# Layer 0 of a four-layer trunk: all 2048 features of the gate product accumulate K chunk by K chunk in eight banks, with shift and scale mostly from VectorE

## The chip, the cores and the metric

The kernel runs on one core of one Trainium2 chip. The metric is the device time of one execution in microseconds (us), taken from outside the profile. Three runs of the kernel before the change took 1386.49, 1388.17 and 1388.37 us; the median is 1388.17.

A core has engines that run their own instruction streams in order and wait for one another by semaphores. In the profile PE is TensorE (matmuls; PEld is its loading of the stationary operand), DVE is VectorE, ACT is ScalarE, POOL is GpSimd, and SP is SyncE, which here only issues DMAs. ACT issues a few DMAs too.

## The reference

The reference is a trunk of four layers on 256 tokens of width 1024. Each layer is a token mixer and a gated FFN with a short convolution. Ahead of each of them stands an RMS norm whose result is scaled and shifted by numbers that a vector c gives through a matrix (`ada_w`). Layer 0 and layer 3 use the gMLP mixer. What matters here is the beginning of layer 0:

```
def rmsnorm(x, g):
    y = xf * lax.rsqrt(jnp.mean(xf * xf, axis=-1, keepdims=True) + EPS)
    return (y * g)
def modulate(h, shift, scale):
    return h * (1.0 + scale[:, None, :]) + shift[:, None, :]

c_act = jax.nn.silu(c)
mod = c_act @ ada_w[i] + ada_b[i]
sh1, sc1, g1, sh2, sc2, g2 = jnp.split(mod, 6, axis=-1)
h = modulate(rmsnorm(x, mix_norm_g[i]), sh1, sc1)

def gmlp_mixer(h, w_in, ln_g, ln_b, w_s, b_s, w_out):
    z = jax.nn.gelu(h @ w_in)
    u, v = jnp.split(z, 2, axis=-1)
    v = layernorm(v, ln_g, ln_b)
    v = v.reshape(B, n, GM_CHUNK, GM_GROUPS, GM_GROUP_DIM)
    ws = jnp.where(mask[None], w_s, jnp.zeros_like(w_s))
    sv = jnp.einsum('gts,bnsgd->bntgd', ws, v) + b_s.T[None, None, :, :, None]
    y = u * sv.reshape(B, S, GM_INNER)
    return y @ w_out
```

`w_in` is 1024 x 4096: u and v have 2048 features each. Shift and scale of the first norm, `sh1` and `sc1`, are 2048 numbers, dot products of c_act with 2048 columns of `ada_w`.

## The kernel before

Activations lie with features on the 128 partitions: x is 8 chunks of 128 features by 256 tokens. Weights stream in units of 1 MB, 128 x 2048, called `raw`. Each half of a unit is split into a rounded part `wh` (a CAST on ACT, L207) and the remainder `wl` (a subtraction on DVE, L208). Each activation is likewise split into `hh` (ACT, L444) and `hlo` (DVE, L445). A product is then three matmuls: hh with wh, hh with wl, hlo with wh (`mm3`, L237).

*The start.* x comes in two halves by SP's queue; cin (c with features on partitions), a piece of the parameters prm, and sel come by ACT's queue. PE runs twelve warmup matmuls. The squares of x are taken by DVE and, for chunks 3 and 7, by ACT (`SQACT`); PE sums them (st), ACT takes the root (sdn, which needs a table load, triggered ahead by a dummy called warm), DVE the reciprocal (rsn), and PE spreads it over all partitions (bcn). For each chunk c of layer 0, `ada_first` (L326) brings 1 MB of `ada_w` and multiplies it on PE with c_act: 32 small matmuls named adaf, 64 in the trace. `first_store` transposes their result on DVE and adds the bias; `mod_post` makes amul = (1 + scale) * g from it. `modulate_chunk` (L438 to L445) then computes nt = x * amul * bcn on DVE, hh on ACT and hlo on DVE. The order of all this in layer 0 is written out by hand in `FIRST` (L39): a is an ada chunk, v a K chunk of the gate product, d a load, p a group of small loads, among them the 512 KB of cbc (c in every partition, with its Silu).

*The gate product.* v has tokens on partitions: 2 halves of 128 tokens by 4 blocks of 512 features, so eight results of 128 x 512, each one bank of PSUM. There are four banks named acc, three named misc and one for ada. `proj_tok_first` (L522) accumulates the first 1024 features K chunk by K chunk in the four acc banks, as the chunks of hh come up. The other two blocks follow with `proj_tok` when all of hh is there. Each result goes through gelu on ACT into v0 or v1, with the sum over features beside it.

*The layer norm of v.* From the sums of three blocks a shift nsh is made; the squares of v (named jk, L575) go through ACT. Gb, ws and bs (layer norm gain, the spatial weights and their bias) are loaded by ACT's queue; POOL spreads the single rows of Gb and bs over the partitions and masks ws (affine select). DVE computes variance, root and reciprocal (vrs), scales ws with it (wsp), and multiplies v with Gb (L623). rsum on PE is a row sum of ws.

*u and go.* Eight units of u follow on PE. To each belongs sv, eight small matmuls of wsp with v (L638), and on DVE gt, u and yl, with `gr`; `go` is the product with w_out, each unit of which adds to x (`residual`) and goes into the sums of squares for the FFN's norm.

*What sets the order.* The program is written engine by engine in one sequence, and a scheduler then fixes each engine's order; `issue_after` holds it at places. The rest of the ada tensors (parts 2 to 5 of layer 0, and all of the other layers) are spread over the program: those in `ADA_P` are adaps matmuls on PE, which also serve as fillers where PE would wait for a norm; those in `ADA_D` are two products per MB on DVE (L315, one custom instruction each, listed as CUSTOM_DVE_ANT_0 in the trace and as ISA in the order). `pace` and `RATE` (L50) say how many of either are loaded per weight unit in each stage. `modulated` (L449) is the norm ahead of all later blocks.

Of the kernel before, what the change touches and what calls it, by code (L numbers as in the profile page):

```python
# [8 lines left out]
F32 = mybir.dt.float32  # L9
# [8 lines left out]
D = 1024  # L18
# [20 lines left out]
FIRST = "a0 d v0 a1 a2 d v1 a3 v2 a4 d v3 a5 v4 a6 d v5 a7 v6 p v7"  # L39
# [10 lines left out]
RATE = {("mix", 0): (0.05, 0.4), ("u", 0): (0.1, 0.9), ("go", 0): (0.35, 0.7), ("up", 0): (0.05, 0.05),  # L50
# [41 lines left out]
def build(ctx, tc, A, out, stages=None):  # L92
# [65 lines left out]

    def late_c():
        with tc.issue_after(state["lastdma"]):  # L160
            nc.sync.dma_start(cbc[:], A["cb"])
        act.activation(cbc[:], cbc[:], AF.Silu)
# [107 lines left out]
    adaps = pp.tile([P, 2, 256], F32, tag="ada", name="adaps", bufs=1)  # L270
# [6 lines left out]
    def ada_tensor(l, u):  # L277


        def load(i):  # L280
# [3 lines left out]
            def run():  # L284
                h = ADA_P.index((l, u)) % 2
                ps = adaps[:, h, :]
# [39 lines left out]
    def ada_first(l, c):  # L326

        raw = wp.tile([P, KC, 4, 64], F32, tag="raw", name=f"adaf{c}", bufs=NRAW)
        nc.sync.dma_start(raw[:].rearrange("p a b c -> p (a b c)"), A["ada0"][l, c])
        ps = misc(f"adaf{c}", (P, 64))  # L330
        with contextlib.ExitStack() as es:
            if "pe" in firsts:
                es.enter_context(tc.issue_after(firsts["pe"]))
            for kc in range(KC):
                for j in range(4):
                    i = pe.matmul(ps[32 * j : 32 * j + 32, :], crep(kc), raw[:, kc, j, :], start=kc == 0, stop=kc == KC - 1,
                                  tile_position=(0, 32 * j))
            firsts["pe"] = getattr(i, "ins", i)
        firsts[c] = ps

    def first_store(l, c):
        tr = t1(f"adaft{c}", 64)
        dve.transpose(tr[:], firsts[c][:])
        for e in range(2):
            b = 8 * e + c
            dve.tensor_tensor(mod[:, l, b : b + 1], tr[:, 32 * e : 32 * e + 1], prm[:, col("ada_b", l * 48 + b) : col("ada_b", l * 48 + b) + 1],
                              op=ALU.add)
        mod_post(l, 8 + c, 1)
# [158 lines left out]
    def proj_tok(blocks, name, sink, b0=0):  # L507

        for b in range(b0, blocks):
# [10 lines left out]
            for t in range(2):  # L520
                sink(b, t, ps[t])

    def proj_tok_first(name, sink, start=None):

        ps = [acc(f"{name}{i}") for i in range(4)]

        def chunk(kc):
            if kc % 2 == 0:
                firsts["w"] = unit(1, 0) if start else unit(2)
# [780 lines left out]
```

## Time and profile before

| | before |
|---|---|
| runs (us) | 1386.49, 1388.17, 1388.37 |
| profiled execution, its own time (us) | 1391.3 |
| its span in the profile (us) | 1389.6 |
| mean granted clock of TensorE | 0.995 |
| first v matmul (us from the span's start) | 11.81 |
| first matmul of u0, end of the v product (us) | 71.29 |
| last go matmul of layer 0 starts (us) | 172.34 |
| first matmul of the FFN's up product in layer 0 (us) | 177.74 |

The profiled execution is a run of its own; its span is the time between the first and the last thing recorded in it. In the rows that follow, a group's row has the line and engine, the operation, out<-in with shapes, the count, then busy us and mean ns, and behind the second bar the idle time of the engine just before these instructions with what ended it. A timeline row has the start, the duration, the engine (ACTq and SPq are the DMA queues of ACT and SP) and the line.

### The profile page before, as it was taken

How to read it: one execution, taken by the hardware profiler on the slowest of the kernel's cores; microseconds unless marked ns; L12 is line 12 of the kernel's file. 1: busy time of each engine (PE TensorE's matmuls, PEld its weight loads, DVE VectorE, ACT ScalarE, POOL GpSimd, SP SyncE). 2: the span in 40 equal slices, each digit the busy share in tenths (PEclk: the TensorE clock that was granted, in tenths of full speed). 3: DMA queues.
4: the chain of work that ended last, by engine and by line, in shares of the span. 5: the costliest groups of instructions: out<-in, count | busy, mean ns of one | idle time of the engine just before them, and what ended most of it. 6: DMA issues, size and time to landing. Idle time of an engine off the chain costs nothing.

```text
span 1389.6 us, 29284 instructions
## 1 busy us (share of the span) xinstructions
PE 1358.8 (98%) x12372; PEld 1286.1 (93%) x12372; DVE 1091.6 (79%) x1760; ACT 770.8 (55%) x1201; POOL 17.2 (1%) x17
## 2 busy tenths in 40 slices
PE   8999999999999999999989999999999999999997
PEld 6799999999987899999987889999987999999997
DVE  5699698889786698897788879889764964888853
ACT  3764366664465566654655646665456653666633
POOL 0100000000000000000010000000001000000000
PEclk9999999999999999999999999999999999999999
DMA  9869955468775276589475577558737465455531
GB/s 383 330 249 337 379 189 214 178 215 346 324 273 213 98 263 245 211 331 372 173 271 194 235 281 296 194 208 322 254 125 258 178 217 182 151 184 182 183 122 31
DMA packets 49483, 326.23 MB, mean 235 GB/s; under 512 B 5956, under 2 KB 9028, under 8 KB 11974
## 3 DMA queue, kind: packets, MB, share of 16 engines
q1 hardware_dynamic: 47568, 322.72, 61.9%
q8 instruction: 97, 1.59, 0.5%
q10 hardware_dynamic: 1784, 1.65, 0.4%
q14 instruction: 34, 0.28, 0.1%
HBM read 323.29 MB, written 1.05 MB: 233 GB/s over the span
## 4 chain that ended last, share of the span: by engine, by line
PE 92%; DVE 3%; DMA 3%; ACT 2%; issue 1%; DVEq 0%; SPq 0%; ACTq 0%
PE up L239 12%; PE up L238 12%; PE up L240 12%; PE dn L238 4%; PE dn L239 4%; PE dn L240 4%; PE go L238 2%; PE go L239 2%; PE go L240 2%; PE u L239 2%; PE u L238 2%; PE u L240 2%; PE adaps L293 2%; PE v L238 2%; PE v L239 2%; PE v L240 2%
## 5 line engine op out<-in xcount | busy, mean ns | idle before, releaser
L207 ACT CAST wh<-raw 128x1024 fp32r<-128x1024 f32 x426 | 434.9, 1031 | 395.5 <-PE up L239 171.4
L208 DVE TENSOR_TENSOR wl<-raw,wh 128x1024 fp32r<-128x1024 f32 x426 | 511.7, 1206 | 162.9 <-ACT wh L207 160.9
L238 PE MATMUL up<-hh,wh 128*128 128x256 f32 x1408 | 398.4, 284 | 2.6 <-ACT hh L444 2.5
L240 PE MATMUL up<-hh,wl 128*128 128x256 f32 x1408 | 398.3, 283 | 0.0
L239 PE MATMUL up<-hlo,wh 128*128 128x256 f32 x1408 | 398.2, 284 | 0.1
L238 PEld LDWEIGHTS up<-hh,wh 128*128 128x128 f32 x1408 | 270.5, 192 | 5.3 <-ACT hh L444 4.5
L239 PEld LDWEIGHTS up<-hlo,wh 128*128 128x128 f32 x1408 | 270.4, 192 | 0.6 <-DVE hlo L445 0.5
L240 PEld LDWEIGHTS up<-hh,wl 128*128 128x128 f32 x1408 | 270.8, 193 | 0.0
L238 PE MATMUL dn<-gh,wh 128*128 128x256 f32 x528 | 149.9, 284 | 1.5 <-ACT y L1089 1.5
L239 PE MATMUL dn<-gl,wh 128*128 128x256 f32 x528 | 149.4, 283 | 0.0
L240 PE MATMUL dn<-gh,wl 128*128 128x256 f32 x528 | 149.4, 283 | 0.0
L315 DVE CUSTOM_DVE_ANT_0 adaw<-adaw,cbc,prm 128x1024 f32<-128x1024 f32 x104 | 131.3, 1276 | 2.2 <-DMA adaw<-adad 2.2
L1089 ACT ACTIVATE y<-up,cwb 128x256 f32<-128x256 f32 x176 | 98.6, 560 | 10.1 <-DVE y L1091 9.8
L238 PEld LDWEIGHTS dn<-gh,wh 128*128 128x128 f32 x528 | 101.3, 192 | 2.0 <-ACT y L1089 1.7
L239 PEld LDWEIGHTS dn<-gl,wh 128*128 128x128 f32 x528 | 101.3, 192 | 0.0
L240 PEld LDWEIGHTS dn<-gh,wl 128*128 128x128 f32 x528 | 101.3, 192 | 0.0
L1091 DVE SCALAR_TENSOR_TENSOR y<-up,cwb,y 128x254 f32<-128x254 f32 x176 | 84.5, 480 | 4.7
L1090 DVE SCALAR_TENSOR_TENSOR y<-up,cwb,y 128x255 f32<-128x255 f32 x176 | 83.9, 477 | 0.8 <-ACT y L1089 0.8
L238 PE MATMUL u<-hh,wh 128*128 128x256 f32 x256 | 73.9, 289 | 0.0
L238 PE MATMUL go<-yh,wh 128*128 128x256 f32 x256 | 73.3, 287 | 0.0
L240 PE MATMUL u<-hh,wl 128*128 128x256 f32 x256 | 72.4, 283 | 0.0
L239 PE MATMUL u<-hlo,wh 128*128 128x256 f32 x256 | 72.4, 283 | 0.0
(337 smaller groups left out, 2478.8 us busy)
## 6 DMA issues: line engine op xcount, KB each, us to landing
raw<-up SPq DMA_DIRECT2D x88, 1024.0 KB, 4.8
adaw<-adad SPq DMA_DIRECT2D x52, 1024.0 KB, 8.1
adaw<-adap SPq DMA_DIRECT2D x36, 1024.0 KB, 7.5
raw<-dn SPq DMA_DIRECT2D x32, 1024.0 KB, 4.8
raw<-gmu SPq DMA_DIRECT2D x16, 1024.0 KB, 4.8
raw<-gmo SPq DMA_DIRECT2D x16, 1024.0 KB, 4.8
raw<-gmv SPq DMA_DIRECT2D x15, 1024.0 KB, 6.3
raw<-dn SPq DMA_DIRECT2D x16, 768.0 KB, 5.5
```

What stands on the lines that cost most here:

```text
L207: act.copy(wh[:, :w], raw[:, o : o + w])
L208: i = dve.tensor_tensor(wl[:, :w], raw[:, o : o + w], wh[:, :w].bitcast(F32), op=ALU.subtract)
L238: pe.matmul(ps, lh, rh, start=start, stop=False)
L239: pe.matmul(ps, lh, rl, start=False, stop=False)
L240: i = pe.matmul(ps, ll, rh, start=False, stop=stop)
L293: pe.matmul(ps[32 * j : 32 * j + 32, :], crep(kc), raw[:, k, j, :], start=kc == 0, stop=kc == KC - 1, tile_position=(0, 32 * j))
L315: dve.tensor_tensor_reduce(raw[:, e, :], raw[:, e, :], cbc[:], 1.0, prm[:, c0 : c0 + 1], ALU.mult, ALU.add, mod[:, l, b : b + 1])
L1089: act.activation(y[:], ps[:, e, :], AF.Identity, bias=b, scale=w[2])
L1090: dve.scalar_tensor_tensor(y[:, 1:], ps[:, e, : S - 1], w[1], y[:, 1:], op0=ALU.mult, op1=ALU.add)
L1091: dve.scalar_tensor_tensor(y[:, 2:], ps[:, e, : S - 2], w[0], y[:, 2:], op0=ALU.mult, op1=ALU.add)
```

## The change

Layer 0's gate product runs in one pass. All four blocks of 512 features accumulate K chunk by K chunk, in eight banks: four acc, three misc, and the bank that the ada matmuls use. So one unit of weights is now one K chunk (all 2048 columns), and gelus, squares and layer norm come when the last chunk is done (`proj_tok_all`).

Shift and scale of layer 0: chunks 0 and 1 stay on PE (`FIRSTPE = 2`). For chunks 2 to 7 the columns lie in the layout of the DVE products, and DVE takes two products of 128 x 1024 per chunk. These need c in every partition at once: one row of c (crow, 1 x 1024) is loaded by ACT's queue, goes through Silu, and POOL spreads it. The 512 KB load of cb and its Silu go. bcn is copied to SBUF (bcs), so that its bank comes free; chunks from 1 on use the copy.

In layer 0 the gating of a unit of u now runs one unit late (`lag = 1`), `pace` for u is given a count, and the rates of u and go are changed.

```diff
-FIRST = "a0 d v0 a1 a2 d v1 a3 v2 a4 d v3 a5 v4 a6 d v5 a7 v6 p v7"
+FIRSTPE = 2
-RATE = {("mix", 0): (0.05, 0.4), ("u", 0): (0.1, 0.9), ("go", 0): (0.35, 0.7), ("up", 0): (0.05, 0.05),
+RATE = {("mix", 0): (0.05, 0.4), ("u", 0): (0.1, 0.75), ("go", 0): (0.35, 0.9), ("up", 0): (0.05, 0.05),
...
     cbc = one.tile([P, D], F32, name="cbc")
-
-    def late_c():
-        with tc.issue_after(state["lastdma"]):
-            nc.sync.dma_start(cbc[:], A["cb"])
-        act.activation(cbc[:], cbc[:], AF.Silu)
+    nc.scalar.dma_start(cbc[0:1, :], A["crow"])
+    act.activation(cbc[0:1, :], cbc[0:1, :], AF.Silu)
+    pool.partition_broadcast(cbc[:], cbc[0:1, :])
...
+    def first_load(l, c):
+
+        raw = wp.tile([P, 2048], F32, tag="raw", name=f"adaf{c}", bufs=NRAW)
+        nc.sync.dma_start(raw[:], A["ada0"][l, c])
+        firsts[c] = raw
+
+    def first_run(l, c):
+        raw = firsts.pop(c)
+        if c >= FIRSTPE:
+
+            v = raw[:].rearrange("p (e k) -> p e k", e=2)
+            for e in range(2):
+                b = 8 * e + c
+                c0 = col("ada_b", l * 48 + b)
+                dve.tensor_tensor_reduce(v[:, e], v[:, e], cbc[:], 1.0, prm[:, c0 : c0 + 1], ALU.mult, ALU.add, mod[:, l, b : b + 1])
+        else:
+            v = raw[:].rearrange("p (k j f) -> p k j f", k=KC, j=4)
+            ps = ada(f"adaf{c}", (P, 64))
+            with contextlib.ExitStack() as es:
+                if "pe" in firsts:
+                    es.enter_context(tc.issue_after(firsts["pe"]))
+                for kc in range(KC):
+                    for j in range(4):
+                        i = pe.matmul(ps[32 * j : 32 * j + 32, :], crep(kc), v[:, kc, j, :], start=kc == 0, stop=kc == KC - 1,
+                                      tile_position=(0, 32 * j))
+                firsts["pe"] = getattr(i, "ins", i)
+            tr = t1(f"adaft{c}", 64)
+            dve.transpose(tr[:], ps[:])
+            for e in range(2):
+                b = 8 * e + c
+                c0 = col("ada_b", l * 48 + b)
+                dve.tensor_tensor(mod[:, l, b : b + 1], tr[:, 32 * e : 32 * e + 1], prm[:, c0 : c0 + 1], op=ALU.add)
         mod_post(l, 8 + c, 1)
 
...
+    def proj_tok_all(l, name, bc0, bc):
+
+        make = [acc] * 4 + [misc] * 3 + [ada]
+        ps = {}
+
+        def products(kc, w, blocks):
             with contextlib.ExitStack() as es:
-                if start and kc < KC - 1:
+                if "pe" in firsts:
                     es.enter_context(tc.issue_after(firsts["pe"]))
-                for b in range(2):
-                    a, bl = hl(firsts["w"], (kc % 2) * 1024 + b * 512, 512)
+                for b in blocks:
+                    a, bl = hl(w, b * 512, 512)
                     for t in range(2):
-                        mm3(ps[2 * b + t][:], hh[:, kc, t * P : t * P + P], hlo[:, kc, t * P : t * P + P], a, bl, kc == 0, kc == KC - 1)
+                        if kc == 0:
+                            ps[b, t] = make[2 * b + t](f"{name}{b}{t}", (P, 512))
+                        mm3(ps[b, t][:], hh[:, kc, t * P : t * P + P], hlo[:, kc, t * P : t * P + P], a, bl, kc == 0, kc == KC - 1)
             firsts["pe"] = state["mm"]
 
-        if start:
-            start(chunk)
-        else:
-            for kc in range(KC):
-                chunk(kc)
-        for i in range(4):
-            sink(i // 2, i % 2, ps[i])
+        modulate_chunk(l, 0, 0, bc0)
+        dma_next()
+        first_load(l, 1)
+        dma_next()
+        first_load(l, 2)
+        for kc in range(KC):
+            w = unit(2) if kc == KC - 1 else unit(1, 0)
+            if kc + 1 < FIRSTPE:
+
+                products(kc, w, (0, 1))
+                first_run(l, kc + 1)
+                products(kc, w, (2,))
+                modulate_chunk(l, 0, kc + 1, bc)
+                products(kc, w, (3,))
+            else:
+                products(kc, w, range(4))
+                if kc < KC - 1:
+                    first_run(l, kc + 1)
+                    modulate_chunk(l, 0, kc + 1, bc)
+            if kc + 2 < KC:
+                dma_next()
+            if kc + 3 < KC:
+                first_load(l, kc + 3)
+            if kc == KC - 3:
+                with tc.issue_after(state["lastdma"]):
+                    nc.sync.dma_start(prm[:, n0:n1], A["prm"][:, n0:n1])
+                conv_load(l)
+        return ps
...
+        nsh = sm("nsh", 2)
+
+        def shift():
+
+            dve.tensor_reduce(nsh[:], sums[:].rearrange("p (t q) -> p t q", t=2)[:, :, 0:3], axis=AX.X, op=ALU.add)
+            dve.tensor_scalar_mul(nsh[:], nsh[:], -4.0 / (3 * GI))
 
...
-        proj_tok_first("v", sink, start)
         if start:
-            pace("mix", l, 20)
-        proj_tok(3, "v", sink, 2)
-
-        nsh = sm("nsh", 2)
+            ps = proj_tok_all(l, "v", *start)
+            for b in range(4):
+                if b == 3:
+                    shift()
+                for t in range(2):
+                    sink(b, t, ps[b, t][:])
+
+            conv_half()
+            conv_half()
+        else:
+            proj_tok_first("v", sink)
+            proj_tok(3, "v", sink, 2)
...
         pool.partition_broadcast(bsf, bsf[0:1, :])
-        proj_tok(4, "v", sink, 3)
...
             dve.tensor_tensor(gt[:], sv[:], r[:].unsqueeze(2).broadcast_to([P, 2, 2, P]), op=ALU.add)
             dve.tensor_tensor(u[:], u[:], gt[:].rearrange("p e t s -> p e (t s)"), op=ALU.mult)
             split(yh(2 * i, 2), yl(2 * i, 2), u[:])
+
+        pace("u", l, *((16,) if start else ()))
+        us = []
+        lag = 1 if start else 0
+        for i in range(8):
+            ps = proj_pair(hk, lk, KC, f"u{i}")
+            if i == 0:
+                state["chain"] = tuple(getattr(s, "ins", s) for j, s in enumerate((warm, rec, root)) if GCH >> j & 1)
+            u = t2("u", (P, 2, S))
+            with tc.issue_after(getattr(root, "ins", root)):
+                act.activation(u[:], ps[:], AF.Gelu_apprx_tanh)
+            us.append((i, u))
+            if len(us) > lag:
+                gating(*us.pop(0))
+        for u in us:
+            gating(*u)
         pace("go", l)
...
                     quick = False
-                    ada_first(l, 0)
+                    first_load(l, 0)
+                    first_run(l, 0)
                     bc0 = rms_bc(cur["st"], D, "n0")
-
...
-                    gmlp(l, l // 3, start)
+                    bcs = big("bcs", (P, S))
+                    act.copy(bcs[:], bc0[:])
+                    gmlp(l, l // 3, (bc0[:], bcs[:]))
...
+    r["crow"] = np.ascontiguousarray(f["c"].reshape(1, D))
+
+
+    a0 = np.ascontiguousarray(aw[:1, :, :2048].reshape(1, KC, P, 2, 8, 4, 32).transpose(0, 4, 2, 1, 5, 3, 6)).reshape(1, 8, P, 2048)
```

**Where instructions now stand.** Two engines at three places, as the programs list them. The first is ACT from the start of the program to the first hh, before:

```order
L152 ACTIVATE cact<-cin 128x8
L1152 ACTIVATE sq_105<-x 128x256 x2
L1155 ACT_TABLE_LOAD
L1155 ACTIVATE warm<-sq_105 128x1
L408 ACTIVATE sdn_184<-st,epsc 128x64
L207 CAST wh_0_212<-raw_209 128x1024
L444 ACTIVATE hh<-nt,mod 128x256
```

and after:

```order
L152 ACTIVATE cact<-cin 128x8
L1220 ACTIVATE sq_107<-x 128x256
L159 ACTIVATE cbc<-cbc 1x1024
L1220 ACTIVATE sq_107<-x 128x256
L1223 ACT_TABLE_LOAD
L1223 ACTIVATE warm<-sq_107 128x1
L421 ACTIVATE sdn_191<-st,epsc 128x64
L205 CAST wh_0_219<-raw_210 128x1024
L1247 COPY bcs<-bcn_195 128x256
L205 CAST wh_1024_223<-raw_210 128x1024
L457 ACTIVATE hh<-nt,mod 128x256
```

The Silu of the row cbc has moved in between the two squares; the copy bcs and a second cast stand ahead of the first hh.

The second place is ACT behind the gate product of layer 0, from the first square jk to the gelu table for u, after:

```order
L637 ACTIVATE jk_627,ss_622<-v0_202,nsh_205 128x512
L637 ACTIVATE jk_629,ss_622<-v1_203,nsh_205 128x512
L637 ACTIVATE jk_631,ss_622<-v0_202,nsh_205 128x512
L637 ACTIVATE jk_633,ss_622<-v1_203,nsh_205 128x512
L643 DMA Gb_635<-gmg 1x2048
L648 DMA ws_638<-gmws 128x1024
L651 DMA bs_640<-gmbs 1x1024
L670 ACT_TABLE_LOAD
L670 ACTIVATE warm_657<-epsc_81 128x1
L637 ACTIVATE jk_659,ss_622<-v0_202,nsh_205 128x512
L637 ACTIVATE jk_661,ss_622<-v1_203,nsh_205 128x512
L660 COPY ws_638<-rsum_644 128x512
```

Before, the three loads stood ahead of the first square, and the last of them there read so:

```order
L591 DMA bs_768<-gmbs 1x1024
L575 ACTIVATE jk_751,ss_748<-v0_193,nsh_747 128x512
L575 ACTIVATE jk_753,ss_748<-v1_194,nsh_747 128x512
L575 ACTIVATE jk_755,ss_748<-v0_193,nsh_747 128x512
L575 ACTIVATE jk_757,ss_748<-v1_194,nsh_747 128x512
```

So the loads of Gb, ws and bs have moved from ahead of the first six squares to behind them.

The third place is DVE at the norm between layer 0's mixer and its FFN, from the last square sq to the first nt, before:

```order
L425 TENSOR_TENSOR sq<-x 128x256
L410 RECIPROCAL rsn_2072<-sdn_2070 128x64
L208 TENSOR_TENSOR wl_0_2120<-raw_1986,wh_0_2119 128x1024
L443 SCALAR_TENSOR_TENSOR nt<-x,amul,bcn_2074 128x256
L143 CAST gmask<-gm_2067 128x192
```

and after:

```order
L438 TENSOR_TENSOR sq<-x 128x256
L318 ISA adaw_4_3_1891,mod<-adaw_4_3_1891,cbc,prm 128x1024
L318 ISA mod 128x1
L423 RECIPROCAL rsn_1859<-sdn_1857 128x64
L318 ISA adaw_4_3_1891,mod<-adaw_4_3_1891,cbc,prm 128x1024
L318 ISA mod 128x1
L206 TENSOR_TENSOR wl_0_1913<-raw_1771,wh_0_1912 128x1024
L143 CAST gmask<-gm_1854 128x192
L254 SCALAR_TENSOR_TENSOR amul<-mod,prm 128x8
L206 TENSOR_TENSOR wl_1024_1941<-raw_1771,wh_1024_1940 128x1024
L456 SCALAR_TENSOR_TENSOR nt<-x,amul,bcn_1861 128x256 x3
```

Two custom products, amul and a second wl have moved in ahead of nt.

More of the change, by code (lines that the diff above doesn't have):

```diff
@@ L324, in build @@
     firsts = {}
[L326 to L333, printed above, removed]
-            for kc in range(KC):
[L335 to L339, printed above, removed]
@@ L624, in gmlp, with gating @@
         yh, yl = hilo("y", 16)
-        pace("u", l)
-        for i in range(8):
-            ps = proj_pair(hk, lk, KC, f"u{i}")
-            if i == 0:
-                state["chain"] = tuple(getattr(s, "ins", s) for j, s in enumerate((warm, rec, root)) if GCH >> j & 1)
-            u = t2("u", (P, 2, S))
-            with tc.issue_after(getattr(root, "ins", root)):
-                act.activation(u[:], ps[:], AF.Gelu_apprx_tanh)
+        def gating(i, u):
             g = i
```

65 lines of the change are left out of this document (23 added, 42 removed).

## The prediction

> **What bounds the kernel now.** I read the page first: busy times, the chain that ended last, the costliest groups.
>
> ```profile
> PE 1358.8 (98%) x12372; PEld 1286.1 (93%) x12372; DVE 1091.6 (79%) x1760; ACT 770.8 (55%) x1201; POOL 17.2 (1%) x17
> PE 92%; DVE 3%; DMA 3%; ACT 2%; issue 1%; DVEq 0%; SPq 0%; ACTq 0%
> L208 DVE TENSOR_TENSOR wl<-raw,wh 128x1024 fp32r<-128x1024 f32 x426 | 511.7, 1206 | 162.9 <-ACT wh L207 160.9
> ```
>
> TensorE is idle for 1389.6 - 1358.8 = 30.8 us. So a gain must come from work taken off TensorE or from those waits, and any new wait of TensorE costs its full length. Next the groups by line of the first 90 us (of 20 to 90 us for ACT and DVE); the first row is what the change takes off TensorE, with its waits at the row's end.
>
> ```profile
> L336 PE MATMUL adaf<-adaf,cact 128*32 128x64 f32 x512 | 8.8, 220 | 3.7 <-DMA adaf<-ada 3.7
> L443 DVE SCALAR_TENSOR_TENSOR nt<-x,amul,bcn 128x256 f32<-128x256 f32 x6 | 2.9, 480 | 0.2
> L561 ACT ACTIVATE v<-v 128x512 f32<-128x512 f32 x8 | 4.7, 595 | 5.2 <-PE v L240 5.1
> L575 ACT ACTIVATE jk<-v,nsh 128x512 f32<-128x512 f32 x8 | 5.7, 714 | 1.2 <-DVE nsh L579 1.1
> L623 DVE SCALAR_TENSOR_TENSOR v<-v,nmu,Gb 128x512 f32<-128x512 f32 x8 | 5.7, 742 | 0.0
> ```
>
> Then the timeline of the start (start, duration), the DMA answer for it (last number: us from issue to landing), and a row of the windows (last two numbers: DMA share, GB/s).
>
> ```profile
> 1.73 0.45 ACTq L131 DMA_DIRECT2D sel<-sel  x1
> 6.39 1.28 ACT L1155 ACT_TABLE_LOAD   x1
> 7.79 0.30 ACT L408 ACTIVATE sdn<-st,epsc 128x64 f32<-128x64 f32 x1
> 8.12 0.55 DVE L410 RECIPROCAL rsn<-sdn 128x64 f32<-128x64 f32 x1 [1.07 <-ACT sdn L408]
> 9.59 1.10 PE L415 MATMUL bcn<-rsn,sel 128*128 128x64 f32 x8
> 11.25 0.51 ACT L444 ACTIVATE hh<-nt,mod 128x256 fp32r<-128x256 f32 x1
> 11.81 0.74 PE L238 MATMUL v<-wh,hh 128*128 128x512 f32 x2 [1.12 <-ACT hh L444]
> cin<-c ACTq DMA_DIRECT2D x1, 4.0 KB, 3.9
> sel<-sel ACTq DMA_DIRECT2D x1, 2.0 KB, 7.0
> 30.00:40.00 10.00, 8.82 (x164) 6.63 (x166) 7.33 (x17) 5.04 (x7) 0.00 (x0) 1.00 1.02 412
> ```
>
> The small loads of ScalarE's queue share the engines with megabytes from SP's queue: cin needed 3.9, and sel, issued third, landed at 1.73 + 7.0 = 8.7. Then the timeline at the end of the gate product v and at the third unit of u:
>
> ```profile
> 71.06 0.39 PE L240 MATMUL v<-wh,hlo 128*128 128x512 f32 x1
> 71.29 0.28 PE L238 MATMUL u<-hh,wh 128*128 128x256 f32 x1
> 84.69 0.36 PE L238 MATMUL u<-hh,wh 128*128 128x256 f32 x1
> ```
>
> Matmuls of v start 0.23 apart, so a K chunk of 24 is 5.5 us. From 71.29 to 84.69 TensorE runs u0, u1 and two sv without a wait, and these 13.4 us cover the layer norm of v.
>
> **The change part by part.** *Removed.* Six of the eight adaf groups leave TensorE. 512 records are 64 a group, the 8.8 us are 1.1 each, and about 1.3 with the change of shape at both ends: 7.7 us, and at most the 3.7 of their waits with it. That is the whole possible gain.
>
> *Start.* ScalarE's queue gets a fourth load, crow, and its Silu stands ahead of the second square, the square-root table and sdn. No row shows crow. Issued at 2.2, it lands at 4.0 if it takes the 1.8 of Gb (rows below), or behind sel, at 9.0. I take 9.0, since it stands behind sel in the same queue. Silu on 1024 elements is 1.06 (row below), the square 0.4, the table 1.28, warm and sdn 0.4, rsn 0.55, bcn 1.1: bcn ends at 13.85 instead of 10.69. The copy bcs is new, and nt waits for it: 0.5 by the hh row of the same shape. With nt 0.5, a cast that now stands ahead of hh, 1.0, and hh 0.5 the first v matmul is at **15.8** against 11.81. With crow at 4.0 it would be 12.6. The broadcast of cbc on POOL lies beside this: VectorE wants cbc only at 23.8.
>
> *K chunks.* Half of chunk 0 (12 x 0.23) and adaf1 end at 19.7. VectorE then does transpose, mod, amul, nt, wl, hlo and wl for chunk 1, 4.1, to 23.8. From chunk 2 on each chunk costs it two custom products (2 x 1.2 back to back, rows below), amul 0.16, nt 0.48, hlo 0.48 and two wl of 1.2, with overlaps **5.9 us**, where TensorE needs 5.5. So VectorE sets the pace: 23.8 + 5 x 5.9 = 53.3, hh of chunk 7 is ready 3.7 later, at 57.0, and v ends at **62.5**, against 71.3. Transfers are close, but don't bind: 2.1 MB a chunk at 412 GB/s is 5.1. SP's queue now waits for crow and sel in places, and these are over by 9.
>
> *After v.* All eight gelus and squares now come behind the last chunk, and ScalarE issues Gb, ws and bs behind the sixth square. What such steps took before:
>
> ```profile
> 39.85 1.06 ACT L162 ACTIVATE cbc<-cbc 128x1024 f32<-128x1024 f32 x1
> 49.41 0.49 ACTq L583 DMA_DIRECT2D Gb<-gmg  x1
> 51.20 2.92 POOL L584 PARTITION_BROADCAST Gb<-Gb  x1 [50.17 <-DMA Gb<-gmg]
> 58.36 1.09 POOL L594 TENSOR_SCALAR_AFFINE_SELECT ws<-ws 128x1024 f32<-128x1024 f32 x1 [4.24 <-DMA ws<-gmws]
> 61.13 1.90 POOL L592 PARTITION_BROADCAST bs<-bs  x1 [1.67 <-DMA bs<-gmbs]
> 48.47 7.72 DVE L208 TENSOR_TENSOR wl<-raw,wh 128x1024 fp32r<-128x1024 f32 x5 [3.44 <-ACT wh L207]
> 58.70 0.77 DVE L579 TENSOR_SCALAR nsh<-nsh 128x2 f32<-128x2 f32 x1
> 59.39 1.27 DVE L315 CUSTOM_DVE_ANT_0 adaw<-adaw,cbc,prm 128x1024 f32<-128x1024 f32 x1
> 60.59 1.27 DVE L315 CUSTOM_DVE_ANT_0 adaw<-adaw,cbc,prm 128x1024 f32<-128x1024 f32 x1
> ```
>
> ScalarE: the gelu table from 58.0, one gelu (59.9), two casts (61.9), seven gelus at 0.58 (65.9), two casts (67.8), six squares at 0.71 (72.0). Its DMA queue may run a few instructions ahead of its compute; I take 70.0 for Gb's issue, 72.0 at the latest. It lands 1.8 later, as at 49.41 to 51.20, and the broadcast ends at 74.7; affine (1.09) and the broadcast of bs (1.90) follow. Meanwhile VectorE wants one custom product and four products of v with Gb (0.66 each back to back). Do these run beside POOL? Under the Gb broadcast five wl took 7.72 instead of 5 x 1.2, and nsh, on 2 elements a row, took 0.77 under affine: VectorE mostly stood still. I take them as exclusive; between 0 and 3.0 us hang on it. Then VectorE goes on at 75.8, behind affine: 1.2 + 2.65 + 1.9 = 81.6. From there variance 0.3, vrs 0.3, gelu table 1.28, gelu, copy and a cast give wh10 at 85.7, and the scaling of ws, two products of v and gr let wl10 end at 86.9. The third u unit could start at **86.8**. In before it started at 84.69, with one sv (0.8) fewer done: comparable is 85.5. TensorE has finished u1 at 74.0 and rsum at 78, so it waits some 6 us.
>
> Such a wait has a price of its own. The longest one of this trace, in the timeline and in windows (the third number from the end is the granted clock):
>
> ```profile
> 724.08 1.94 PE L937 MATMUL psum<-hsg,ones 128*32 128x512 f32 x8 [3.52 <-DVE hsg L953]
> 728.67 0.63 PE L240 MATMUL hi<-wh,hlo 128*128 128x512 f32 x1
> 729.10 0.63 PE L238 MATMUL hi<-wh,hh 128*128 128x512 f32 x1
> 725.00:728.00 3.00, 3.00 (x13) 1.67 (x6) 3.00 (x4) 0.00 (x0) 0.00 (x0) 0.50 1.08 415
> 730.00:732.00 2.00, 2.00 (x15) 1.10 (x14) 0.52 (x1) 1.05 (x1) 0.00 (x0) 1.00 0.22 90
> ```
>
> After 3.52 us of waiting the granted clock was 0.50, with matmuls 0.43 apart instead of 0.23, until about 730, 5.9 us after work came back. So sv0 to sv2, 2.4 us from 84.0 on, would take 4.9, and u2 starts at **88.9**. Bounds: 0, and half of 5.9, 2.9; I take 2.1. The Trainium skill, page "TensorE: Matmul & The Clock Gate", Part 1, has this as a rule: an idle window of about 3.4 us halves TensorE's clock, and some 3.4 us of sustained work give it back. By the page the loss here would be 1.3 (an estimate) and the sum 0.8 lower; this trace's half clock lasted longer.
>
> *Boundary to the first FFN.* By the new rates adaw0_4_3 is loaded later. Its two custom products now stand on VectorE among the steps of the norm, and amul, which needs them, and a second wl come ahead of nt.
>
> ```profile
> 173.18 0.42 DVE L425 TENSOR_TENSOR sq<-x 128x256 f32<-128x256 f32 x1
> 174.48 0.55 DVE L410 RECIPROCAL rsn<-sdn 128x64 f32<-128x64 f32 x1 [0.88 <-ACT sdn L408]
> 175.41 1.23 DVE L208 TENSOR_TENSOR wl<-raw,wh 128x1024 fp32r<-128x1024 f32 x1 [0.38 <-ACT wh L207]
> 176.56 0.47 DVE L443 SCALAR_TENSOR_TENSOR nt<-x,amul,bcn 128x256 f32<-128x256 f32 x1
> 177.74 0.51 PE L238 MATMUL up<-hh,wh 128*128 128x256 f32 x2
> ```
>
> The first product fits into the 0.88 of idle time but for 0.4. The second (1.2), amul (0.16) and wl (1.2) push nt, and with it hh and up, **2.9** later in all. TensorE's fillers here, the adaps, are 48 matmuls before and after, and before they lasted just until up; so the 2.9 are a wait. If the products come through ahead of sq, it is 0. At the other boundaries the fillers differ by 8 adaps (0.5 us) in either direction; I take 0, give or take 0.8.
>
> **Sum.** 88.9 - 85.5 = 3.4, and 2.9: +6.3, which is 1397.6 beside the profiled execution's own 1391.3. That execution lies 3.1 above the median of the runs, 1388.17, from which I start: **1394.5**.
>
> **Rivals.** *A: crow lands early*, 3.9 after issue like cin, at 6.1. For it: it is one row of 4 KB. Against it: sel's 7.0, on the same queue. First v at 12.9 and all that follows 2.9 earlier: +3.4, 1391.6.
>
> *B, not slower: POOL's work is ready in time.* ScalarE's queue issues Gb so far ahead of the squares that POOL is done before VectorE needs Gb. Then the last square, at 75.1, decides, and variance to wl10 add 5.3: u2 at 80.4, 5.1 earlier than before, with too short a wait for the half clock. With the boundary -2.2: 1386.0. It holds if Gb is issued by 66. Against it: at 49.41 Gb went out among the casts at its own place, not far ahead.
>
> *C: A and B together*, -2.2 - 2.9 = -5.1: 1383.1.
>
> *D: half clock at two more places.* At the start TensorE is idle from 7.5 to 10.4, while st waits for the second square, and at the FFN for 2.9; the clock may fall in both. For it: half a clock for 5.9 us takes 2.9 at the FFN, and bcn at half clock 1.0 at the start. Against it: the one fall that I see took 3.5 of waiting. +10.2, 1398.4.
>
> *E: VectorE's loop is hidden.* If 5.9 a chunk is too high and TensorE's 5.5 sets the pace, v ends 2.2 earlier: +4.1, 1392.3. Against it: the sum of the rows.
>
> **How the numbers follow.** Chances: forecast 0.36, A 0.12, B 0.16, C 0.13, D 0.15, E 0.08. A measurement of this kernel can tell about 0.2%, 2.8 us, from no change: 1385.4 to 1391.0 counts as the same. Slower: forecast, D, E and half of A (0.06), 0.65. Same: the other half of A and most of B (0.13), 0.19. Faster: C and the rest of B (0.03), 0.16. The range leaves out C and the far end of D: 1385.0 to 1399.5. The forecast's own range is 1392 to 1397.
>
> **What would show it.** The Silu of crow starting near 9 and the first v matmul near 15.8; VectorE with hardly any idle time between 24 and 53; v ending near 62.5; POOL's broadcast of Gb starting past 71; TensorE idle for about 6 us ahead of sv0 and a granted clock of 0.5 behind it; at the FFN, up starting 2.9 later after the last go matmul than before. I am wrong if crow lands by 5, if Gb is broadcast before 70, if u2 starts before 84, or if up follows go as closely as before.

## The result, and the profile after

The changed kernel takes 1405.20 us (median of four runs, 1404.86 to 1405.66), the kernel before 1388.27 beside it (four runs, 1386.49 to 1389.01): a ratio of 1.0123, 95% interval 1.0110 to 1.0135. It is slower by 16.9 us, where +6.3 was forecast, and it lies above the range's end of 1399.5. The profiled execution took 1405.02, its span is 1403.3. One run of all, 3534.68 us in the experiment with 832 columns below, was disturbed and is left out.

The page of the changed kernel, busy times (and instructions) of each engine:

```profile
PE 1362.6 (97%) x11988; PEld 1288.1 (92%) x11988; DVE 1103.6 (79%) x1766; ACT 768.0 (55%) x1201; POOL 18.2 (1%) x18
```

TensorE has 384 matmul records fewer (12372 - 11988, the six adaf groups) and yet 3.8 us more busy time, and it is idle for 1403.3 - 1362.6 = 40.7 us instead of 30.8. Fewer matmuls that are busy for longer go with the lower clock: the mean granted clock is 0.987 instead of 0.995. The longest waits of TensorE in the changed kernel (engine, line, what was waited for: total, times, longest):

```profile
PE rsum L659 <- POOL ws L655: 4.3, 1, 4.3
PE up L236 <- ACT hh L457: 4.0, 2, 2.5
PE gram L998 <- issue: 4.0, 2, 2.0
PE st L413 <- ACT sq L1220: 3.0, 1, 3.0
PE up L236 <- DVE y L1161: 2.4, 6, 0.4
PE sv L692 <- DVE wsp L680: 2.4, 1, 2.4
PE dn L236 <- DVE y L1161: 2.1, 1, 2.1
```

They lie at five places: the start (st), the end of v (rsum, sv), the first feed-forward (the 2.5 of up), layer 1's feed-forward (up and dn behind y), and layer 2's mixer (gram, which waits 3.1 in the kernel before, too). The timeline of the changed kernel (start, duration) at the first three, and two hh of the K loop:

```profile
8.98 1.05 ACT L159 ACTIVATE cbc<-cbc 1x1024 f32<-1x1024 f32 x1 [3.78 <-DMA cbc<-crow]
12.70 1.97 PE L428 MATMUL bcn<-rsn,sel 128*128 128x64 f32 x8 [0.16 <-DVE rsn L423]
16.48 0.79 PE L236 MATMUL v<-wh,hh 128*128 128x512 f32 x1 [1.81 <-ACT hh L457]
...
40.81 0.51 ACT L457 ACTIVATE hh<-nt,mod 128x256 fp32r<-128x256 f32 x1 [3.47 <-DVE nt L456]
46.68 0.51 ACT L457 ACTIVATE hh<-nt,mod 128x256 fp32r<-128x256 f32 x1 [3.46 <-DVE nt L456]
...
64.59 0.28 PE L236 MATMUL u<-hh,wh 128*128 128x256 f32 x1
...
71.83 0.23 ACTq L643 DMA_DIRECT2D Gb<-gmg  x1
76.28 2.30 POOL L644 PARTITION_BROADCAST Gb<-Gb  x1 [64.86 <-DMA Gb<-gmg]
76.94 2.58 DVE L318 CUSTOM_DVE_ANT_0 adaw<-adaw,cbc,prm 128x1024 f32<-128x1024 f32 x1 [2.74 <-DMA adaw<-adad]
78.42 2.04 POOL L655 TENSOR_SCALAR_AFFINE_SELECT ws<-ws 128x1024 f32<-128x1024 f32 x1
79.45 4.45 DVE L684 SCALAR_TENSOR_TENSOR v<-v,nmu,Gb 128x512 f32<-128x512 f32 x4
80.52 3.52 PE L659 MATMUL rsum<-ws,ones 128*128 128x512 f32 x4 [4.26 <-POOL ws L655]
85.28 0.15 DVE L677 RECIPROCAL vrs<-vrs 128x2 f32<-128x2 f32 x1
86.40 3.09 PE L692 MATMUL sv<-wsp,v 128*128 128x128 f32 x18 [2.36 <-DVE wsp L680]
...
177.90 0.48 DVE L472 SCALAR_TENSOR_TENSOR x<-go,gate,x 128x256 f32<-128x256 f32 x1 [4.58 <-PE go L238]
178.76 1.28 DVE L318 CUSTOM_DVE_ANT_0 adaw<-adaw,cbc,prm 128x1024 f32<-128x1024 f32 x1
180.43 1.19 DVE L318 CUSTOM_DVE_ANT_0 adaw<-adaw,cbc,prm 128x1024 f32<-128x1024 f32 x1
185.21 0.62 PE L236 MATMUL up<-hh,wh 128*128 128x256 f32 x3 [2.48 <-ACT hh L457]
```

The reader sees every mechanism that the prediction named: the Silu of crow at 9, the hh 5.87 us apart, the late Gb, VectorE's product of adaw stretched from 1.28 to 2.58 under POOL's broadcast, TensorE waiting twice ahead of sv, and up 7.31 us behind the last x (177.90 to 185.21). In the kernel before up came 5.08 behind it:

```profile
172.66 0.48 DVE L459 SCALAR_TENSOR_TENSOR x<-go,gate,x 128x256 f32<-128x256 f32 x1 [4.58 <-PE go L240]
```

That is 177.74 - 172.66. The windows of the changed kernel behind v and at the feed-forward (third number from the end: granted clock):

```profile
80.00:82.00 2.00, 1.48 (x2) 0.64 (x3) 2.00 (x2) 0.00 (x0) 2.00 (x2) 0.71 0.00 0
82.00:84.00 2.00, 2.00 (x3) 0.34 (x1) 2.00 (x5) 0.59 (x1) 0.17 (x1) 0.50 0.00 0
88.00:90.00 2.00, 2.00 (x11) 2.00 (x11) 2.00 (x4) 2.00 (x4) 0.00 (x0) 0.50 0.00 0
188.00:190.00 2.00, 2.00 (x11) 2.00 (x11) 2.00 (x6) 0.94 (x3) 0.00 (x0) 0.50 0.65 274
```

The clock was halved behind the waits for ws (rsum), for wsp (sv) and for hh (up). In the trace it is also halved from 9.15 to 19.39, behind the wait of st, and in windows of layers 2 and 3; behind the waits for y it is not.

Then the same milestones of both traces were set side by side, the first and the last x that a product has updated in each stage. The changed kernel is behind by 5.60 us at the first go (132.89 and 138.49), 5.24 at the last go, 8.91 at the end of layer 0's feed-forward, 10.83 and 15.25 at the ends of layer 1's mixer and feed-forward, 13.1 behind layer 2's mixer, and 13.7 at the end. So 8.9 us arise in layer 0, where 6.3 were predicted, and 4.8 behind it, where nothing was predicted. (In layer 2's mixer the changed kernel gains 2.1: the wait of 3.52 that the prediction shows there, with two windows at half clock behind it, is not in its trace.) The remaining 3.2 of the 16.9 are the kernel before's own profiled execution, 3.0 slower than the median of its runs, while that of the changed kernel stands at its median.

### The profile page after: what moved, and what is told of

It reads as the page before. It is cut to its first block, busy times and chain, and to the rows that moved or that the text cites. A ratio compares the mean times of both kernels' runs of the same rounds, so it can differ in the third digit from the quotient of the medians.

```text
span 1403.3 us, 28547 instructions
## 1 busy us (share of the span) xinstructions
PE 1362.6 (97%) x11988; PEld 1288.1 (92%) x11988; DVE 1103.6 (79%) x1766; ACT 768.0 (55%) x1201; POOL 18.2 (1%) x18
## 3 DMA queue, kind: packets, MB, share of 16 engines
q8 instruction: 94, 1.54, 0.4%
## 4 chain that ended last, share of the span: by engine, by line
PE 89%; DVE 5%; ACT 2%; DMA 1%; issue 1%; ACTq 0%; DVEq 0%; SPq 0%
PE up L236 12%; PE up L237 12%; PE up L238 12%; PE dn L236 4%; PE dn L237 4%; PE dn L238 4%; PE go L236 2%; PE go L237 2%; PE go L238 2%; PE adaps L296 2%; PE u L236 2%; PE u L237 2%; PE u L238 2%; DVE wl L206 2%; PE v L236 1%
```

## The experiments

Each is timed against the kernel before, whose median was 1389.0 to 1389.3 in the three batches. The changed kernel was not timed again beside them; "less than the changed kernel" is against its 1405.20, when the kernel before took 1388.27.

**The start: crow first on ScalarE's queue.**

```
+    cbc = one.tile([P, D], F32, name="cbc")
+    nc.scalar.dma_start(cbc[0:1, :], A["crow"])
     cin = one.tile([P, 8], F32, name="cin")
...
-    cbc = one.tile([P, D], F32, name="cbc")
-    nc.scalar.dma_start(cbc[0:1, :], A["crow"])
     act.activation(cbc[0:1, :], cbc[0:1, :], AF.Silu)
```

> Only change against the changed kernel: crow is issued first on ScalarE's queue instead of fourth. Theory (the start is paid because the Silu of crow holds the second square): crow lands by about 4.5, its Silu runs from about 4.8 to 6.2, first v matmul at about 12.9 instead of 16.48, the granted clock stays full through the first 20 us, and adaf1 ends about 5 us earlier; as the K chunks go at VectorE's pace, everything behind follows: about 1400.2, 5 us less than the changed kernel's 1405.2 (3.4 to 6). Rival (the later stages are held by something with a time of its own, the transfers of the weights or of adaw0_2_1): the first v matmul moves as far, but u2 by less than 2 us, 1403 or more.

Measured: 1403.29 (1400.44 to 1405.36), ratio 1.0107 (1.0087 to 1.0127): 1.9 less than the changed kernel. Its timeline:

```profile
4.02 1.06 ACT L159 ACTIVATE cbc<-cbc 1x1024 f32<-1x1024 f32 x1
13.85 0.79 PE L236 MATMUL v<-wh,hh 128*128 128x512 f32 x1 [1.94 <-ACT hh L457]
18.70 0.63 PE L238 MATMUL v<-wh,hlo 128*128 128x512 f32 x1
19.26 1.27 PE L352 MATMUL adaf<-adaf,cact 128*32 128x64 f32 x64
```

The Silu comes 5 us earlier and the first v 2.6 earlier, but the second chunk's adaf only 1.5 earlier (19.26 instead of 20.78): all of chunk 0's products now run at half clock (each takes 0.63; in the changed kernel they take 0.39 from 19.5 on). v ends 1.3 earlier, vrs also 1.3, go's first x 1.6, but the third unit of u only 0.7 (88.48 instead of 89.14). So the theory holds for the first v alone. The full clock that it counted on did not come: this trace has half clock from 12.85 to 19.68, and again from 77.70 to 87.94. Total and third unit of u lie where the rival put them, but its reason is not borne out, since vrs moves by as much as the end of v: nothing with a time of its own held it there. The 1.9 in total are not clear of noise by themselves: the intervals of the two ratios overlap.

**After v: Gb, ws and bs issued behind the last chunk's hh.**

```
         if start:
             ps = proj_tok_all(l, "v", *start)
+            with tc.issue_after(state["hh"]):
+                Gb, wr, ws, rsum, bs = loads()
...
+            if start and i == 1:
+                rsums()
```

`loads()` holds the three DMAs and POOL's two broadcasts, `rsums()` the row sum, now behind u1; state["hh"] is the last hh.

> Against the changed kernel: Gb, ws and bs are issued right behind the last chunk's hh instead of behind the sixth square, and rsum stands behind u1 in the program. Theory (the broadcasts on GpSimd and their quarrel with VectorE hold the third unit of u): GpSimd is done with Gb by about 66 and with bs by about 72, the eight products of v with Gb take 0.66 to 0.74 each instead of 1.1, vrs comes at about 78.2 instead of 84.79, the third unit of u starts at about 82.2 instead of 89 to 91, and there is no half clock behind it: about 1397.5, 7.5 us less (6 to 9). Rival (adaw0_2_1's landing at 76.9, for which VectorE waited, or ScalarE's chain of gelus and squares, holds it): vrs comes no earlier than 82, 1402 or more.

Measured: 1397.05 (1395.84 to 1400.39), ratio 1.0072 (1.0051 to 1.0093): 8.2 less. Its timeline:

```profile
59.02 0.23 ACTq L622 DMA_DIRECT2D Gb<-gmg  x1
63.53 2.55 POOL L623 PARTITION_BROADCAST Gb<-Gb  x1 [51.98 <-DMA Gb<-gmg]
71.95 1.28 DVE L318 CUSTOM_DVE_ANT_0 adaw<-adaw,cbc,prm 128x1024 f32<-128x1024 f32 x1
74.20 3.40 DVE L698 SCALAR_TENSOR_TENSOR v<-v,nmu,Gb 128x512 f32<-128x512 f32 x5
79.23 0.16 DVE L691 RECIPROCAL vrs<-vrs 128x2 f32<-128x2 f32 x1
79.96 2.05 PE L706 MATMUL sv<-wsp,v 128*128 128x128 f32 x16 [1.45 <-DVE wsp L694]
```

Confirmed. With POOL done by 69 VectorE's product takes 1.28 again and a v product 3.40 / 5 = 0.68 instead of 4.45 / 4 = 1.11; sv starts at 79.96 instead of 86.40, and from v to the boundary (177.4) no window is at half clock. The Trainium skill, page "SBUF — State Buffer", section "Who interferes with whom", states that a VectorE instruction with two inputs in SBUF contends with a GpSimd instruction that reads SBUF, for a port pair that is locked exclusively. The two traces agree as far as the lengths go (2.58 and 1.28, 1.11 and 0.68). Gb still takes 63.53 - 59.02 = 4.5 from issue to broadcast, as in the changed kernel (76.28 - 71.83).

**The clock after v: TensorE kept busy.**

```
+            if start and i == 1:
+                keep = ada("keep", (P, P))
+                with tc.issue_after(state["mm"]):
+                    for n in range(36):
+                        pe.matmul(keep[:], onesw[:], onesw[:], start=True, stop=True)
```

> The changed kernel with 36 matmuls of the constant ones behind layer 0's u1: 27 ahead of rsum and 9 behind it, so that TensorE is busy while it waits for ws and for wsp. Theory: the half clock at 80.8 and 87.7 comes from the idle stretches of 4.3 and 2.4 us, so the granted clock stays at 1.00 from 76 to 92, sv still starts at 86.4 +- 0.5, and what follows it gains the 1.7 us that half of a 3.41 us window costs: u2's milestones and go0 1.7 earlier, 1403.5. Rival 1: the clock falls without idleness, the same windows at 0.50, 1405 to 1406. Rival 2: the clock stays up here but the window turns up later, so the total is within 0.5 of 1405.2.

Measured: 1401.70 (1400.44 to 1402.88), ratio 1.0093 (1.0080 to 1.0106): 3.5 less. Its windows and its timeline:

```profile
82.00:84.00 2.00, 2.00 (x9) 1.04 (x8) 2.00 (x5) 0.59 (x1) 0.12 (x1) 1.00 0.00 0
88.00:90.00 2.00, 2.00 (x18) 1.89 (x17) 2.00 (x3) 2.00 (x3) 0.00 (x0) 1.00 0.00 0
```

```profile
76.22 6.19 PE L717 MATMUL keep<-ones 128*128 128x128 f32 x54
82.25 1.88 PE L659 MATMUL rsum<-ws,ones 128*128 128x512 f32 x4
86.36 1.83 PE L692 MATMUL sv<-wsp,v 128*128 128x128 f32 x14 [0.22 <-DVE wsp L680]
```

TensorE does 36 matmuls (72 records) more, nothing that it waits for comes earlier (sv at 86.36 and 86.40), and the kernel is faster. The clock stayed at 1.00, rsum took 1.88 instead of 3.52, and go's first x came 1.3 earlier, where 1.7 was expected. So here idleness brings the half clock. The rest of the gain lies elsewhere: behind it each stage matches the changed kernel's to within 0.5 us (1.1 together) up to layer 2's mixer, which took 152.8 instead of 156.5; there the changed kernel's trace has two windows of 3.41 us at half clock (at 763.5 and 777.1) and this one none (1.4 of it is lost again in layer 3's feed-forward, to a second window there). The shift in time changed where such windows fall; that this is a matter of phase is argued, not shown.

**What paces the K loop.** First VectorE's products were halved.

```
-                dve.tensor_tensor_reduce(v[:, e], v[:, e], cbc[:], 1.0, ...
+                dve.tensor_tensor_reduce(v[:, e, :512], v[:, e, :512], cbc[:, :512], 1.0, ...
```

> The changed kernel with VectorE's products for chunks 2 to 7 over 512 of the 1024 columns (half of each sum is left out, the loads stay as they are). VectorE then works some 4.7 us a chunk, TensorE's 24 matmuls need 5.43. Theory, VectorE paces the K loop: v ends near 62.6 instead of 64.6 (TensorE's own floor: 16.5 + 8 x 5.43 + 1.1 for the second chunk's adaf + 1.6 at half clock), about 1403.2. Rival, the loads pace it as much (two of 1 MB per 5.9 us is 355 GB/s, the DMA share reads 0.94 to 1.02 in each 6 us window from 28 to 64): v still ends between 64.2 and 64.8 and VectorE now waits for DMA, 1405.

Measured: 1408.35 (1405.92 to 1409.97), ratio 1.0140 (1.0127 to 1.0153), v ends at 65.56: neither theory. The waits of VectorE in this kernel, from 28 to 58 us:

```profile
DVE hlo L458 <- ACT hh L457: 2.9, 5, 0.6
DVE wl L206 <- ACT wh L205: 2.3, 5, 0.5
```

VectorE waits for ScalarE, never for a DMA: with the shorter products the scheduler had put hh ahead of two casts on ScalarE, and the round trip of hh, casts, wl and nt took 5.94 a chunk. The order had changed with the size, so the run could not answer. With 832 columns the order on all engines is that of the changed kernel:

> The changed kernel with VectorE's products for chunks 2 to 7 over 832 of the 1024 columns (the rest of each sum is left out, the loads stay as they are). The instructions stand in the same order on VectorE, ScalarE and TensorE as in the changed kernel, which with 512 columns they did not. Each of the twelve products takes 0.23 us less, so VectorE's own work falls from 5.87 to 5.42 us a chunk, TensorE's 24 matmuls need 5.43. Theory, VectorE paces the K loop: the hh of chunks 3 to 7 follow each other by 5.42 to 5.5 instead of 5.87, the last hh comes some 2 us earlier (56.4 instead of 58.4), v ends 1.5 to 2 earlier, and the total lies near 1403.5. Rival, the loads pace it (two of 1 MB per 5.87 us): the spacing stays at 5.8 to 5.9 and VectorE waits for DMA or ScalarE, total 1405.

Measured: 1402.11 to 1404.53 in three runs, ratio 1.0100 (1.0075 to 1.0125). Two hh of this kernel:

```profile
45.42 0.51 ACT L457 ACTIVATE hh<-nt,mod 128x256 fp32r<-128x256 f32 x1 [3.06 <-DVE nt L456]
50.90 0.51 ACT L457 ACTIVATE hh<-nt,mod 128x256 fp32r<-128x256 f32 x1 [3.07 <-DVE nt L456]
63.07 0.28 PE L236 MATMUL u<-hh,wh 128*128 128x256 f32 x1
```

5.47 apart instead of 5.87, and v ends 1.5 earlier. In the changed kernel's own trace VectorE waits for nothing from 28 to 58 us. So VectorE sets the pace in the changed kernel; rival E, that its loop is hidden, falls. (The total, 1.0100, is not clear of the changed kernel's 1.0123; the spacing is what decides.) The loads, though busy throughout, keep up with 5.47.

**Behind layer 0: the planner's accumulators.** The planner has one accumulator for each kind of ada load ("p" for TensorE's, "d" for VectorE's). Each unit adds the stage's RATE to them, and one load goes out for each whole one reached. They carry over from stage to stage. In front of layer 0's feed-forward they stand at 0.35 and 1.0 in the kernel before, at 0.15 and 0.4 in the changed one. Three kernels: the old values put back in the changed kernel; the same and the old rate for u, which brings adaw0_4_3 back ahead of the norm; and the new values alone in the kernel before.

```
             pace("up", l, 33, "big")
+            if l == 0:
+                state["p"], state["d"] = 0.34999999999999987, 0.9999999999999998
```

> Against the changed kernel: one line sets the two accumulators that pace the loads of the ada tensors, at the beginning of layer 0's FFN, to the values that they had there in the kernel before, so that from there on nearly every ada load stands where it stood before; layer 0's mixer and its boundary stay as in the changed kernel. Theory (part of the loss is scattered over layers 1 to 3, because the ada work was shifted there by these accumulators): of the 13.7 us between the two traces 4.8 arise behind layer 0's FFN, and these go: about 1400.4 (1399.5 to 1402). Rival (that part is due to where the clock's windows fall, or is the same in any kernel that starts late): 1404 or more.

```
-RATE = {("mix", 0): (0.05, 0.4), ("u", 0): (0.1, 0.75), ...
+RATE = {("mix", 0): (0.05, 0.4), ("u", 0): (0.1, 0.9), ...
```

> As the run with the accumulators set, and besides the rate of u is 0.9 instead of 0.75, so that adaw0_4_3 is loaded and multiplied ahead of the last square of layer 0's norm. Theory (VectorE's two products, amul and wl ahead of nt make the boundary 3.7 us longer, 2.5 of waiting and the rest by half clock): the time from the last go matmul to up is the 5.1 us of before, and the total is lower by 3.7 than with the accumulators alone: about 1396.7 (1395.5 to 1398). Rival (the boundary is long for another reason, hh on ScalarE or the fillers): no more than 1 us lower than with the accumulators alone.

```
             pace("up", l, 33, "big")
+            if l == 0:
+                state["p"], state["d"] = 0.15, 0.4
```

> The kernel before with one line added: the accumulators of the planner's pace stand at 0.15 and 0.4 in front of layer 0's feed-forward, as the changed kernel leaves them there, instead of 0.35 and 1.0. Up to that line it is the kernel before, word for word; behind it its loads stand as in the changed kernel. Theory: the carried accumulators cost what the stages behind layer 0's feed-forward lost in the changed kernel: +4.8, 1393.8, with layer 1's mixer +1.9 and its feed-forward +4. Rival: the loss needs the changed kernel's late boundary as well: 1389 to 1390.

Measured: 1400.28 (1396.17 to 1400.77), ratio 1.0080 (1.0061 to 1.0099), 4.9 less than the changed kernel; with the rate 1397.01 (1393.24 to 1397.79), ratio 1.0058 (1.0039 to 1.0076), 8.2 less, with up 5.08 behind the last x as in the kernel before; and the kernel before with the line 1396.64 (1392.88 to 1398.94), ratio 1.0060 (1.0048 to 1.0072): 7.5 slower, where 4.8 was expected. The first two came as their theories had them. TensorE's waits and groups in layer 1's feed-forward, first of the kernel before (463 to 652 us):

```profile
PE up L238 <- ACT hh L444: 1.5, 1, 1.5
L293 PE MATMUL adaps<-adaw,cact 128*32 128x256 f32 x54 | 3.7, 382 | 0.0
```

then the group of the changed kernel (474 to 667 us), where all the waits behind y of its list above lie:

```profile
L296 PE MATMUL adaps<-adaw,cact 128*32 128x256 f32 x70 | 4.8, 383 | 0.6 <-DVE adat L261 0.6
```

of the changed kernel with the old values put back (474 to 661 us):

```profile
L296 PE MATMUL adaps<-adaw,cact 128*32 128x256 f32 x54 | 3.7, 382 | 0.0
```

and of the kernel before with the one line (464 to 657 us):

```profile
PE up L238 <- DVE y L1091: 2.4, 6, 0.4
PE dn L238 <- DVE y L1091: 2.1, 1, 2.1
L293 PE MATMUL adaps<-adaw,cact 128*32 128x256 f32 x70 | 4.8, 383 | 0.6 <-DVE adat L263 0.6
```

One line that touches no computation brings the changed kernel's times in layer 1 to the kernel before, and the same line with the old values takes them away again. 16 records of adaps more stand in this feed-forward, and VectorE, with the moved products of adaw on it, delivers y late to up and dn. The stage takes 191.9 us in the changed kernel and in the kernel before with the line, 187.6 in the kernel before and in the changed kernel with the old values; layer 1's mixer 90.7 against 88.8. (Both traces with 187.6 hold a window at half clock there, at 470.5 and at 481.8; the two with 191.9 hold none.) With the old values put back, the time from the end of layer 0 to the end of the program is 6.5 less than in the changed kernel's trace. The rival, that the late boundary is needed for this, falls.

What the line costs in the kernel before is less sure than that it costs. Its runs go with their clock: 1392.9 at a mean granted clock of 0.997, 1394.7 at 0.996, 1398.5 to 1398.9 at 0.993 to 0.990. At 0.997 there is one run of it, and three of the kernel before, 1387.1 to 1387.7: 5 to 6 us. Span against span the two traces differ by only 1.6, because layer 2's mixer takes 153.9 with the line and 158.7 without it, in a trace that has the wait of 3.52 and its two windows there. Where its longer runs lose their time is not shown; the one trace of it is of the shortest.

**All three repairs together.**

> The changed kernel with all three repairs at once: the c row loaded first on ScalarE's queue, Gb/ws/bs issued behind the last chunk's hh with rsum behind u1, and the accumulators and layer 0's u rate as the kernel before has them in front of the feed-forward. Theory: the four costs lie one behind the other on TensorE's path, so the gains add: 1405.2 - 1.9 - 8.2 - 8.2 = 1386.9, a little below the kernel before (1389.0); vrs near 77.2, x's first eighth behind the mixer (go0) near 130.6, up 5.1 behind the last x. Rival 1, the gains overlap (the boundary's stall and the late u2 wait for the same adaws): two thirds of the sum, 1392 to 1394. Rival 2, the K-chunk order itself costs: not below 1389.

Measured: 1385.58 (1383.88 to 1389.22, eight runs) beside 1389.10 (14 runs): ratio 0.9979 (0.9970 to 0.9989). Its timeline where v is normalised:

```profile
77.50 0.15 DVE L691 RECIPROCAL vrs<-vrs 128x2 f32<-128x2 f32 x1
78.22 2.05 PE L706 MATMUL sv<-wsp,v 128*128 128x128 f32 x16 [1.59 <-DVE wsp L694]
```

The gains add: 1386.9 was expected; vrs comes at 77.50 (77.2 expected) and sv 8.2 earlier than in the changed kernel, up comes 5.14 behind the last x, and go's first x at 130.45, 2.4 ahead of the kernel before. This version is faster than both kernels, by 3.5 us than the one before. So the K-chunk order was not what made the change slow; three things that came with it were. Both rivals fall.

## Why the prediction was wrong, point by point

The sign was right and the mechanisms of layer 0 were right; the size was 10.6 us short: 2.6 in layer 0, 4.8 behind it, and 3.2 in the starting point.

| step | predicted | measured |
|---|---|---|
| Silu of crow; first v | 9.0; 15.8 | 8.98; 16.48 |
| K loop per chunk; last hh; end of v | 5.9; 57.0; 62.5 | 5.87; 58.41; 64.59 |
| Gb issued; broadcast starts | 70.0; 71.8 | 71.83; 76.28 |
| first go against before | +3.4 | +5.6 |
| last go to the end of the first feed-forward | +2.9 | +3.7 |
| behind layer 0's feed-forward | 0 | +4.8 |
| profiled execution of before against its runs | carried over | 3.2 more |

**Start: right, mis-sized by the clock.** The order on ScalarE came as forecast, but bcn took 1.97 instead of 1.10, since the wait for st had halved the clock: the part of rival D at the start. Rivals A and C, crow early, fall with the Silu at 8.98. Chunk 0's products and adaf1 took 5.4 (16.48 to 21.88) where 3.9 were counted (15.8 to 19.7), also at half clock. The two, 0.7 and 1.5, make up v's delay of 2.1, less 0.1 that the loop won.

**K loop: right.** The pace is VectorE's, as the run with 832 columns shows.

**After v: right, mis-sized in the transfer, and near in one number by luck.** That POOL and VectorE hold each other up, with "between 0 and 3.0" hanging on it, is borne out. But the landing of Gb was taken at 1.8 us from one row, and it is 4.5 here and in the experiment: the row of before (issued at 49.41, broadcast at 51.20) was no price for it. The issue came at 71.83, near the late bound of 72.0. So the broadcast ended at 78.6 instead of 74.7. The first sv came at 86.40, where the working had 84.0. Yet u2 came at 89.14, where 88.9 was forecast: three sv at half clock, 4.9 us, were to run ahead of u2, and only 18 of their 24 records did, in 2.7. Two errors cancelled there, and the first go is still 2.2 later than forecast. With 18 records instead of 24 the time of the kernel before to compare u2 with is 84.9, not 85.5 (0.6); the half clock goes on behind u2 until 91.06 (1.0, half of what is left of the window); go's first x comes 8.8 behind go's first matmul instead of 8.3 (0.5). Rival B, POOL ready in time, needed an issue by 66 and did not happen; but the experiment with an issue at 59.02 shows that its mechanism was right, too: sv then starts 6.4 earlier.

**Boundary: right, but for the clock.** Both products of adaw0_4_3 stand on VectorE behind sq, up comes 2.2 later (2.9 forecast), and behind the wait stands a window at half clock, up to 1.7 us. Rival D alone had this window.

**Behind layer 0: the step that failed.** It read: "At the other boundaries the fillers differ by 8 adaps (0.5 us) in either direction; I take 0, give or take 0.8." The boundaries were looked at by the count of their fillers alone. What differs is the state that the planner carries out of layer 0, and with it every later ada load; the cost sits inside layer 1's mixer (1.9) and feed-forward (4.2), where no boundary was looked at. The two kernels with the one line show it: the old values take 4.9 us off the changed kernel, and the new ones cost the kernel before 7.5 by the medians, 5 to 6 at equal clock.

**The sum's starting point.** Adding the difference to the median took it for granted that the 3.1 us by which before's profiled execution lay above its runs would be in the changed kernel's, too. They were not: the changed kernel's four runs lie within 0.7 us of its profiled one, all at 0.987. That trace of before has windows at half clock (470.5 for 3.41 us and 723.1 for 6.83), but these do not explain all of the 3.1, since seven runs of the kernel before in the later batches, at the same clock of 0.995, took 1387.7 to 1389.9. Why the changed kernel's runs vary so little and those of the kernel before with the accumulator line by 6 us stays open.

## What to carry to other kernels

When a change touches a planner's rate or the number of units in one stage, look at the state that the planner carries out of that stage, and compare the order of loads to the end of the program, not only around the edit. A small transfer that a chain waits for belongs at the earliest place its queue allows, and its landing time is not to be taken from one row. A wait of TensorE of some 2 us can cost twice, its length and half clock behind it, up to 1.7 us for each window of 3.41; look at the granted clock, since not every such wait brings one.

## What the runs showed of the hardware

The half clock comes in windows of 3.41 us or multiples of it (3.41, 6.83, 10.24 and 13.65 in these traces), and waits shorter than that were followed by one: 2.36 ahead of sv at 86.40, with half clock from 87.7, and 2.48 ahead of up at 185.21, with half clock from 186.6, each for 3.41 us. The length of the wait alone does not decide: 1.54 at 468.20 in the kernel before was followed by half clock, 2.69 at 758.58 in the kernel with the 36 matmuls was not. What decides stays open. The Trainium skill, page "TensorE: Matmul & The Clock Gate", Part 1, names an idle window of about 3.4 us as the condition and a free-running window; the length agrees, the waits here were shorter. 36 matmuls without any use went with a kernel faster by 3.5 us, 1.3 of it at the place where they stand. And the run times of the kernel before with the one line go with the mean granted clock, by some 6 us between 0.997 and 0.990, so that a profile's time has to be put beside those of the runs before a few us are read from it.
